# Where a two-layer hybrid kernel loads its modulation weights: token stores behind the first norm's weights, later modulation rows beside the second pair's features

## The chip, the cores and the metric

One Trainium2 chip, one core. The metric is the device time of one execution in microseconds, the median over several runs. Engine names are the profile's: PE is TensorE's matmul, PEld its weight load, DVE is VectorE, ACT ScalarE, POOL GpSimd, SP the engine whose queue issues every DMA of this kernel.

## What is computed

Two trunk layers work on 1024 latent and 256 context tokens of width 1024. In each layer a condition vector gives 3072 modulation numbers for the latent tokens and 3072 for the context (shift, scale, gate); the tokens are normalised and modulated, projected, mixed by a retention head group and an RWKV-7 head group, projected out, and added to the residual times the gate.

```python
def adaln(cond, w_mod, b_mod):
    m = jax.nn.silu(cond.astype(jnp.float32)) @ w_mod + b_mod
    return jnp.split(m, 3, axis=-1)
...
    for layer in range(DEPTH):
        sh_l, sc_l, g_l = adaln(c, w_mod[layer], b_mod[layer])
        sh_c, sc_c, g_c = adaln(c_ctx, w_mod[layer], b_mod[layer])
        hl = rms_norm(xl, norm_w[layer]) * (1.0 + sc_l[:, None]) + sh_l[:, None]
        hc = rms_norm(xc, norm_w[layer]) * (1.0 + sc_c) + sh_c
        pl = hl @ w_in[layer]
        pc = hc @ w_in[layer]
...
        xl = xl + g_l[:, None] * mix_l
```

`w_mod[layer]` is 1024 by 3072 float32, 12 MB; both layers' make 24 MB, in the kernel three blocks of 8 MB.

## The kernel before

Tokens lie as 10 tiles of 128 (tiles 0 and 1 are context). The kernel writes program order by hand, and a scheduler then moves instructions on each engine's queue: it starts what is ready in its own timeline and prefers what was written earlier, so an instruction may run well ahead of its place in the program. On the chip each engine works its queue in order.

**The modulation rows.** `adaln` (L270 to L295) multiplies the two condition vectors with one 8 MB block of `w_mod`. For each of 8 row blocks it loads a `wm` tile of 128x2048 (1 MB, L277) and makes four products of 2x512 into the bank `pmod` (L280); the profile shows each product as two passes. I call the four products of one `wm` tile a group. The four write different partitions of the bank and run side by side, so a group or half of one takes about the same time. Then `pmodT` (L289) turns the rows into columns. It is called three times: block one, shift and scale of layer 0, inside the first norm (L454); block two, the gates of both layers (L1145); block three, shift and scale of layer 1 (L1146). The `wm` tiles have three buffers (`WMB`).

**The start of layer 0.** Token tiles are loaded (`xt`, L167), transposed into `xs` (`pxt`, L451), and each of the three `xs` chunks is stored to DRAM once (`xd<-xs`, 1, 2 and 2 MB, L459), for the residual at the layer's end. `norm_chunk` (L341 to L365) writes the normalised tokens as two half-precision parts, `h_hi` and `h_lo`. Then `lora` (L682 to L691) projects 128 columns (`pproj`, L486 to L488: five pieces of 24 products), and `features(0)` (L734 to L784) projects the keys, receptances and values of the first head pair, with the `zstage` (`pz`, L696 to L724) merged into the receptances. Projection weights come through `w_block` (L322 to L334): a load `wraw`, two ACT passes and one POOL pass into `whi` and `wlo`, each with two buffers. Then the scan begins.

**The scan.** Four head pairs of ten steps make 40 steps a layer. `seq` (products `pseq`, L1044 and L1052) and the preparation `prep2` have high priority. Between the steps `deal` hands out other work from two streams: `stream` (features, gates and retention of the pairs, through `feats`) and `out_stream` (the output projection, `pout`). The pair `DENSE[l]` says how much work, in microseconds of PE, each stream holds; `deal` spreads it over the steps left.

Of the kernel before, what the change touches and what calls it, by code (L numbers as in the profile page):

```python
# [10 lines left out]
F32 = mybir.dt.float32  # L11
# [3 lines left out]
ALU = mybir.AluOpType  # L15
# [39 lines left out]
WMB = 3  # L55
# [1 line left out]
RETW = 32  # L57
NTM = (5, 7)
XB = 4
DENSE = ((447.0, 113.0), (403.0, 88.0))  # L60
DUE = (30, 37)


# [62 lines left out]
def hybrid_kernel(ctx: ExitStack, tc: tile.TileContext, a: dict, out: bass.AP, dbg: dict | None = None):  # L126
    nc = tc.nc
# [14 lines left out]
    def pj(name="pj"):  # L142
        return bank("pj", name)

    load = nc.sync.dma_start

    def behind(ins, first):
        tc.add_manual_dep(ins.ins, first.ins.name, mybir.DependencyInfo(mybir.DependencyClass.NoSync, mybir.DependencyReason.DATA),
                          reason="the first product of a bank clears its written bits")

    open_pools = {}

# [55 lines left out]
    at = {}  # L208
# [34 lines left out]
    x_v = x_d.rearrange("k p t -> p k t")  # L243
# [16 lines left out]
    silu = const.tile([128, 16], F32, name="silu")  # L260
# [6 lines left out]
        nc.vector.scalar_tensor_tensor(silu, th, 1.0, p[:, 0:16], ALU.add, ALU.mult)  # L267
        nc.vector.tensor_scalar(silu, silu, 0.5, None, ALU.mult)

    def adaln(pool, spans, tag):  # L270

        pt = bank(tag, "pmod")
        for k in range(8):
            wm = pool.tile([128, 2048], F32, tag="wm", name="wm", bufs=WMB)
            n = 0
            for l, b0, nb in spans:
                load(wm[:, 512 * n:512 * (n + nb)], a["w_mod"][l, 128 * k:128 * k + 128, 512 * b0:512 * (b0 + nb)])  # L277
                n += nb
            for n in range(4):
                nc.tensor.matmul(pt[32 * n:32 * n + 2, :], silu[:, k:16:8], wm[:, 512 * n:512 * n + 512],  # L280
                                 start=(k == 0), stop=(k == 7))
        ms = pool.tile([128, 512], F32, tag="ms", name="ms", bufs=2)
        nc.gpsimd.memset(ms, 0.0)
        for n in range(4):
            r = slice(32 * n, 32 * n + 2)
            (nc.scalar.copy if n % 2 else nc.vector.tensor_copy)(ms[r], pt[r])
        p2 = bank(tag, "pmodT")
        for j in range(4):
            nc.tensor.transpose(p2[:, 128 * j:128 * j + 128], ms[:, 128 * j:128 * j + 128], ident)  # L289
        n = 0  # L290
        for l, b0, nb in spans:
            v = p2.rearrange("p (j n c) -> p c n j", j=4, c=32)[:, 0:2, n:n + nb]
            n += nb
            for c in range(2):
                nc.vector.tensor_copy(modr[l][:, c, 4 * b0:4 * (b0 + nb)].rearrange("p (n j) -> p n j", j=4), v[:, c])  # L295

    def merge(x, nx, y, ny):

# [75 lines left out]
    for l in range(DEPTH):  # L374
# [55 lines left out]
        if l == 0:  # L430
            lp = ln_pool
            stage = [lp.tile([128, 8, 128 * len(tiles)], F32, name=f"xs{ci}") for ci, tiles in enumerate(LN_TILES)]
            for ci, tiles in enumerate(LN_TILES):
                nt = len(tiles)
                rs = lay.tile([128, 4], F32, tag=f"rs{ci}", name="rs")
                hs = lp.tile([128, 4, 2], F32, tag="hs", name="hs", bufs=2)
                rss[ci] = rs
                xt = []
                for i, tb in enumerate(tiles):
                    t = x_tiles[tb] if tb < XTB else x_tile(tb)  # L440
                    for q in range(2):
                        junk = lp.tile([128, 512], F32, tag="ntm", name="junk", bufs=NTM[0])
                        nc.scalar.activation(junk, t[:, 512 * q:512 * q + 512], AF.Square, accum_out=hs[:, i, q:q + 1])
                    xt.append(t)
                nc.vector.tensor_tensor(rs[:, 0:nt], hs[:, 0:nt, 0], hs[:, 0:nt, 1], ALU.add)
                nc.vector.tensor_scalar(rs[:, 0:nt], rs[:, 0:nt], 1.0 / D, EPS, ALU.mult, ALU.add)
                pow_mhalf(rs[:, 0:nt], rs[:, 0:nt])
                for k in range(8):
                    p = bank(("inv", "m")[k % 2], "pxt")
                    for i, t in enumerate(xt):  # L450
                        nc.tensor.transpose(p[:, 128 * i:128 * i + 128], t[:, 128 * k:128 * k + 128], ident)  # L451
                    (nc.scalar.copy if k % 2 else nc.vector.tensor_copy)(stage[ci][:, k, :], p[:, 0:128 * nt])
                if ci == 0:
                    adaln(lp, [(0, 0, 4)], "sq")  # L454
            mod = dict(A=modulation(8, 8, "A", True), B=modulation(0, 8, "B", False))
            for ci, tiles in enumerate(LN_TILES):
                norm_chunk(lp, l, h, mod, tiles, rss.pop(ci), lambda k: stage[ci][:, k, :])
            for tiles, x in zip(LN_TILES, stage):
                load(x_v[:, :, 128 * tiles[0]:128 * tiles[-1] + 128], x)  # L459
            lv32 = lp.tile([128, 768], F32, tag="xt", name="lv32", bufs=XTB)  # L460
            load(lv32, a["c_lv"])
            nc.vector.tensor_copy(lvm.rearrange("p d n t -> p (d n t)"), lv32)
        else:
            mod = dict(A=modulation(8, 8, "A", True), B=modulation(0, 8, "B", False))
            lp = open_pool("nm", side)
            for tiles in OUT_TILES:
                x = xres.pop(tiles[0])
                norm_chunk(lp, l, h, mod, tiles, rss.pop(tiles[0]), lambda k: x[:, k, :])
            close_pool("nm")
            close_pool("xl")  # L470
            close_pool("xa")
            close_pool("ow")
# [334 lines left out]
        def out_sum(x, tiles, k, parts):  # L807

            c = 1 if tiles[0] < 2 else 0
            p = pj("pout")[:, 0:128 * len(tiles)]  # L810
            for i, ((hi, lo), (mh, ml)) in enumerate(parts):
                nc.tensor.matmul(p, hi, mh, start=(i == 0), stop=False)  # L812
                nc.tensor.matmul(p, hi, ml, start=False, stop=False)  # L813
                nc.tensor.matmul(p, lo, mh, start=False, stop=(i == len(parts) - 1))  # L814
            nc.vector.scalar_tensor_tensor(x, p, gmod[:, c, k:k + 1], x, ALU.mult, ALU.add)

        def out_part(chunks, key, stay):

# [322 lines left out]

        for _ in lora():
            pass
        if l == 0:
            adaln(lp, [(0, 4, 2), (1, 4, 2)], "inv")  # L1145
            adaln(lp, [(1, 0, 4)], "sq")  # L1146
        for _ in features(0):
            pass
        if l == 0:
            close_pool("ln")  # L1150
        gmod = modulation(16, 8, "G", False)

        def feats(p):
            yield from gates(p)
            gated.add(p)
            if p + 1 < NP:
                yield from merge(zstage(p + 1), 4.3, features(p + 1), 44)
                ready.add(p + 1)
            else:
                yield from ret_keys(p, cs[p])  # L1160
# [38 lines left out]
        fills = [stream(), out_stream()]  # L1199
        left = list(DENSE[l])  # L1200

# [23 lines left out]
        sp = open_pool("scan", other)  # L1225
# [79 lines left out]
```

## Time and profile before

| | |
|---|---|
| median of 3 runs (lowest to highest) | 2474.76 us (2469.43 to 2476.56) |
| profiled execution, its own time | 2457.0 us |
| its span, first to last instruction | 2455.2 us |
| PE busy | 2291.1 us, 93% |
| VectorE busy | 1735.0 us, 71% |
| ScalarE busy | 1416.7 us, 58% |
| GpSimd busy | 1321.3 us, 54% |
| mean granted TensorE clock | 0.968 |
| HBM read, written | 212.21 MB, 85.98 MB |

Each row of a timeline has a start and a duration in microseconds, the engine, the line, what is written and read, the shape, and in brackets how long the engine had been idle before it and what ended that. A matmul's duration is its latency; matmuls overlap, so their rate is read from the distance of their starts. The granted clock is a share of full speed: 1.00 is 2.4 GHz, 0.50 is 1.2 GHz, and a mean between them is a mix of the two in time.

### The profile page before, as it was taken

What the parts mean: (1) busy time and instruction counts of PE and PEld (TensorE: products, weight loads), DVE (VectorE), ACT (ScalarE), POOL (GpSimd) and SP (SyncE); (2) the same over time, 40 slices, a digit from 0 to 9 for tenths busy, and PEclk for the clock granted to TensorE, in tenths of its full rate; (3) what the DMA queues carried; (4) which work ended last, traced back from release to release, by engine and by line L of the source; (5) the groups of instructions that cost most, each with busy time, mean ns of one, the idle gap of its engine ahead of it and who ended that gap; (6) DMA issues with size and microseconds to landing.
All of it is one profiled execution on the core that took longest, in us unless ns stands there. A gap on an engine that the chain in (4) does not pass through costs nothing.

```text
span 2455.2 us, 69588 instructions
## 1 busy us (share of the span) xinstructions
PE 2291.1 (93%) x25463; PEld 1730.3 (70%) x25463; DVE 1735.0 (71%) x4784; ACT 1416.7 (58%) x4261; POOL 1321.3 (54%) x2032
## 2 busy tenths in 40 slices
PE   5778999999999999999996899999999999998997
PEld 2357776877688777778655687678768867776855
DVE  2656676787678867787648678767867876768756
ACT  3455664565566655566546666646655665556663
POOL 1455564465546644556536566545654665456662
PEclk7889999999999999999998899999999999999999
DMA  8754343344334423346543544334433443234544
GB/s 309 270 191 116 112 119 85 110 111 127 79 87 133 134 68 94 76 110 163 160 123 108 155 126 115 105 94 119 126 87 102 124 115 85 75 96 120 143 131 129
DMA packets 539606, 302.77 MB, mean 123 GB/s; under 512 B 238995, under 2 KB 526465, under 8 KB 537217
## 3 DMA queue, kind: packets, MB, share of 16 engines
q1 hardware_dynamic: 539264, 298.33, 42.3%
q8 instruction: 201, 3.29, 0.6%
q14 instruction: 141, 1.15, 0.2%
HBM read 212.21 MB, written 85.98 MB: 121 GB/s over the span
## 4 chain that ended last, share of the span: by engine, by line
PE 63%; DVE 12%; DMA 5%; ACT 3%; issue 3%; POOL 2%; SPq 1%; DVEq 0%; POOLq 0%; ACTq 0%
PE pproj L486 9%; PE pproj L488 9%; PE pproj L487 8%; PE pseq L1052 8%; PE pm L953 5%; PE pinv L992 2%; PE pseq L1044 2%; PE pinv L1008 2%; PE pout L812 2%; PE pout L814 2%; PE pout L813 1%; PE pss L629 1%; PE pkt L588 1%; PE pss L639 1%; PE pbt L960 1%
## 5 line engine op out<-in xcount | busy, mean ns | idle before, releaser
L486 PE MATMUL pproj<-h_hi,whi 128*128 128x256 f16 (+2 forms) x2128 | 630.2, 298 | 14.0 <-ACT h_hi L364 8.5
L487 PE MATMUL pproj<-h_lo,whi 128*128 128x256 f16 (+2 forms) x2128 | 628.1, 297 | 6.1 <-DVE h_lo L365 5.6
L488 PE MATMUL pproj<-h_hi,wlo 128*128 128x256 f16 (+2 forms) x2128 | 626.9, 297 | 1.0 <-POOL wlo L320 1.0
L320 POOL TENSOR_TENSOR wlo<-wraw,whi 128x256 f16<-128x256 f32 x360 | 250.3, 707 | 210.2 <-ACT wraw L319 186.0
L486 PEld LDWEIGHTS <-whi 128*128 128x128 f16 x2128 | 212.5, 100 | 83.1 <-issue 18.8
L488 PEld LDWEIGHTS <-wlo 128*128 128x128 f16 x2128 | 213.2, 100 | 75.4 <-issue 10.9
L487 PEld LDWEIGHTS <-whi 128*128 128x128 f16 x2128 | 212.4, 100 | 74.7 <-issue 16.5
L977 POOL COPY ttb<-tt 64x256 f16<-64x256 f16 x320 | 139.0, 435 | 203.1 <-DVE tt L1012 155.7
L1006 DVE TENSOR_TENSOR xx<-pinv,lvm 128x256 f16<-128x256 f32 x400 | 163.8, 415 | 94.0 <-PE pinv L992 90.8
L318 ACT ACTIVATE whi<-wraw 128x256 f16<-128x256 f32 x360 | 138.8, 411 | 132.1 <-PE pproj L487 61.0
L1009 ACT CAST tz<-pinv 128x256 f16<-128x256 f32 x400 | 146.0, 371 | 117.2 <-PE pinv L1008 105.9
L953 PE MATMUL pm<-own,bk 64*128 64x128 f32 (+1 forms) x1280 | 198.9, 291 | 8.0 <-DVE bk L933 4.1
L1012 DVE STREAM_TRANSPOSE tt<-tz 128x256 f16<-128x256 f16 x320 | 139.3, 437 | 92.0 <-ACT tz L1009 87.3
L967 POOL TENSOR_TENSOR il<-gq,c_id 64x256 f32<-64x256 f32 x160 | 120.5, 753 | 133.3 <-DVE gq L956 114.7
L977 ACT COPY ttb<-tt 64x256 f16<-64x256 f16 x320 | 128.6, 402 | 101.3 <-DVE tt L1012 96.5
L953 PEld LDWEIGHTS pm<-own,bk 64*128 64x128 f32 x1280 | 160.8, 190 | 33.2 <-issue 9.5
L956 DVE TENSOR_TENSOR gq<-pm,c_m 128x256 f32<-128x256 f32 (+1 forms) x320 | 115.5, 401 | 47.7 <-PE pm L953 46.7
L1052 PE MATMUL pseq<-st,own 64*64 64x64 f32 x2432 | 148.9, 227 | 0.0
L319 ACT ACTIVATE wraw<-wraw 128x256 f32<-128x256 f32 x376 | 146.4, 410 | 3.9
L1003 POOL TENSOR_TENSOR lo<-il,hi 64x256 f16<-64x256 f32 x160 | 113.3, 708 | 35.9 <-ACT hi L968 24.8
L992 PEld LDWEIGHTS <-hi 128*128 128x128 f16 x1920 | 104.0, 99 | 39.6 <-issue 9.3
L1008 PE MATMUL pinv<-xx,ttb 128*128 128x64 f16 x1600 | 112.8, 194 | 11.7 <-DVE xx L1006 9.4
(255 smaller groups left out, 5897.9 us busy)
## 6 DMA issues: line engine op xcount, KB each, us to landing
ft<-feat SPq DMA_DIRECT2D x320, 160.0 KB
wraw<-in_w_in_dram SPq DMA_DIRECT2D x264, 128.0 KB
feat<-zth SPq DMA_DIRECT2D x80, 256.0 KB
wm<-in_w_mod_dram SPq DMA_DIRECT2D x16, 1024.0 KB
wraw<-in_w_out_dram SPq DMA_DIRECT2D x112, 128.0 KB
lap<-la SPq DMA_DIRECT2D x40, 256.0 KB
uv<-vt SPq DMA_DIRECT2D x320, 32.0 KB
wm<-in_w_mod_dram SPq DMA_DIRECT2D x16, 512.0 KB
```

The costliest lines, as they stand in the source:

```text
L319: nc.scalar.activation(raw, raw, AF.Copy, scale=WS)
L320: nc.gpsimd.tensor_tensor(lo, raw, hi, ALU.subtract)
L486: nc.tensor.matmul(p[:, 0:n], hi[:, k, :], h_hi[:, kk, m0:m1], start=first, stop=False)
L487: nc.tensor.matmul(p[:, 0:n], hi[:, k, :], h_lo[:, kk, m0:m1], start=False, stop=False)
L488: nc.tensor.matmul(p[:, 0:n], lo[:, k, :], h_hi[:, kk, m0:m1], start=False, stop=stop)
L953: nc.tensor.matmul(pm[h][:, i, d, 0:q1], bk[HR[h], i, d, :], own[HR[h], i, d, 0:q1], start=True, stop=True)
L977: eng(idr(dst[HR[h], :, :, 64 * h:64 * h + 64]), idr(src[HR[h]]))
L992: nc.tensor.matmul(q[:, i, d, :], hi[:, i, d, :], id16 if n == 0 else tz[:, i, d, :], start=True, stop=True)
L1006: nc.vector.tensor_tensor(xx, q, mk, ALU.mult)
L1008: nc.tensor.matmul(tp[:, i, d, :], ttb[:, i, d, :], xx[:, i, d, :], start=True, stop=True)
L1009: nc.scalar.copy(tzn, tp)
L1052: rm = nc.tensor.matmul(pq[HR[h], k, d, :], lhs, rhs, start=False, stop=stop, skip_group_check=True)
```

## The change

Two things move. The three stores of `xs` get an ordering to the last `pmod` product of block one, which concerns the order of the queue and adds no wait. Blocks two and three leave their place ahead of `features(0)` and become a generator, `gate_rows`, merged with the second pair's features; their `wm` tiles come from the scan's pool with two buffers instead of three, their bank is `rt` instead of `inv` and `sq`, and `modulation(16, ...)` (the gates) moves with them. `DENSE[0]` grows by the 9 units that the generator yields.

```diff
-DENSE = ((447.0, 113.0), (403.0, 88.0))
+DENSE = ((456.0, 113.0), (403.0, 88.0))
...
-    def adaln(pool, spans, tag):
+    def adaln(pool, spans, tag, bufs):
...
-            wm = pool.tile([128, 2048], F32, tag="wm", name="wm", bufs=WMB)
+            wm = pool.tile([128, 2048], F32, tag="wm", name="wm", bufs=bufs)
...
-                nc.tensor.matmul(pt[32 * n:32 * n + 2, :], silu[:, k:16:8], wm[:, 512 * n:512 * n + 512],
-                                 start=(k == 0), stop=(k == 7))
-        ms = pool.tile([128, 512], F32, tag="ms", name="ms", bufs=2)
+                at["pmod"] = nc.tensor.matmul(pt[32 * n:32 * n + 2, :], silu[:, k:16:8], wm[:, 512 * n:512 * n + 512],
+                                              start=(k == 0), stop=(k == 7))
+            yield 0.5
+        ms = pool.tile([128, 512], F32, tag="ms", name="ms", bufs=1)
...
             for tiles, x in zip(LN_TILES, stage):
-                load(x_v[:, :, 128 * tiles[0]:128 * tiles[-1] + 128], x)
+                behind(load(x_v[:, :, 128 * tiles[0]:128 * tiles[-1] + 128], x), at["pmod"],
+                       "the weights of the modulation go first")
...
-        if l == 0:
-            adaln(lp, [(0, 4, 2), (1, 4, 2)], "inv")
-            adaln(lp, [(1, 0, 4)], "sq")
         for _ in features(0):
             pass
         if l == 0:
             close_pool("ln")
-        gmod = modulation(16, 8, "G", False)
+        gmod = []
+
+        def gate_rows():
+
+            if l == 0:
+                yield from adaln(sp, [(0, 4, 2), (1, 4, 2)], "rt", 2)
+                yield from adaln(sp, [(1, 0, 4)], "rt", 2)
+            gmod.append(modulation(16, 8, "G", False))
...
-                yield from merge(zstage(p + 1), 4.3, features(p + 1), 44)
+                wide = merge(zstage(p + 1), 4.3, features(p + 1), 44)
+                yield from wide if p else merge(gate_rows(), 9 if l == 0 else 1, wide, 48)
```

The built order shows where the scheduler puts them. First, SP's queue in the first norm, before:

```order
L277 DMA wm<-in_w_mod_dram 128x2048
L167 DMA xt<-in_x_dram 128x1024 x2
L459 DMA xd<-xs_175 128x8x256
L277 DMA wm<-in_w_mod_dram 128x2048
```

and after the change, from the last four `wm` tiles of block one:

```order
L277 DMA wm<-in_w_mod_dram 128x2048 x2
L167 DMA xt<-in_x_dram 128x1024 x4
L334 DMA wraw<-in_w_in_dram 128x2x128
L462 DMA xd<-xs_175 128x8x256
L462 DMA xd<-xs_176 128x8x512
L465 DMA lv_565<-in_c_lv_dram 128x768
L462 DMA xd<-xs_177 128x8x512
L693 DMA la<-la 64x256 x4
L712 DMA lap<-la 128x2x256
L693 DMA la<-la 64x256 x4
L277 DMA wm<-in_w_mod_dram 128x1024 x4
```

The 1 MB store has gone from between the weights of block one to behind its last token tiles, and the first weights of block two stand behind the stores of `lora`'s first two pieces, where before six of its eight tiles stood ahead of them.

Second, PE's queue around block three. Before, its first groups follow block two in the middle of the key projection of `features(0)`:

```order
L280 MATMUL pmod<-wm,silu 2x512 x4
L289 MATMUL pmodT<-c_id,ms 128x128 x4
L280 MATMUL pmod<-wm,silu 2x512 x8
L486 LDWEIGHTS whi
L486 MATMUL pproj<-h_hi,whi 128x256
```

After, they stand in the receptance projection, among the `pks` products of the keys and the `pz` products:

```order
L290 MATMUL pmodT<-c_id,ms 128x128 x4
L756 MATMUL pks<-c_id,rn 64x128 x4
L280 MATMUL pmod<-wm,silu 2x512 x8
L749 MATMUL pks<-bones_111,psq 128x2 x2
L756 MATMUL pks<-c_id,rn 64x128 x4
L280 MATMUL pmod<-wm,silu 2x512 x4
L720 LDWEIGHTS wz
L720 MATMUL pz<-lh,wz 128x256
```

and the SP queue that feeds them is

```order
L277 DMA wm<-in_w_mod_dram 128x2048 x2
L712 DMA lap<-la 128x2x256
L760 DMA feat_115<-pkp 128x256
L727 DMA feat_115<-zth 128x2x256 x2
L760 DMA feat_115<-pkp 128x256
L277 DMA wm<-in_w_mod_dram 128x2048 x2
```

So block two now lies in the key projection and block three in the receptance projection of the first pair: later than before, yet still ahead of the first scan step but for one group, and not beside the second pair's features. Each `wm` load of block three stands behind stores of results that PE's own products make.

Third, PE's queue at the last `pseq` of layer 0. Before:

```order
L814 MATMUL pout<-mh,wll 128x512
L1052 MATMUL pseq<-uv,gq 64x64 x4
L881 MATMUL pxo<-c_id,x_18738 128x128
L812 LDWEIGHTS wlh
L812 MATMUL pout<-mh,wlh 128x512
```

After:

```order
L818 MATMUL pout<-mh,wll 128x512
L885 MATMUL pxo<-c_id,x_18738 128x128
L1056 MATMUL pseq<-uv,gq 64x64 x4
L885 MATMUL pxo<-c_id,x_18738 128x128
L816 LDWEIGHTS whi
L816 MATMUL pout<-mh,whi 128x256
```

Behind the last `pseq` and ahead of layer 1's first projection stood 120 `pout` products (96 of 128x256, 24 of 128x512); now 345 stand there (216 and 129), among them the main part of the output projection, which reads `whi`.

## Rows read from the trace of the kernel before

**Rows 1.** The page's parts 1 and 2: busy time, then slices of 61 us.

```profile
PE 2291.1 (93%) x25463; PEld 1730.3 (70%) x25463; DVE 1735.0 (71%) x4784; ACT 1416.7 (58%) x4261; POOL 1321.3 (54%) x2032
...
PE   5778999999999999999996899999999999998997
...
PEclk7889999999999999999998899999999999999999
```

**Rows 2.** Busy by stretch: PE, PEld, DVE, ACT, POOL; PEclk, DMA share, GB/s.

```profile
67.00:92.00 25.00, 18.31 (x88) 6.54 (x88) 24.84 (x29) 13.21 (x26) 20.52 (x15) 0.77 0.69 253
92.00:140.00 48.00, 43.44 (x318) 22.76 (x316) 17.32 (x37) 18.28 (x45) 7.95 (x11) 0.90 0.76 274
140.00:182.00 42.00, 29.77 (x214) 22.05 (x213) 23.88 (x53) 21.58 (x66) 25.55 (x45) 0.84 0.52 151
182.00:205.00 23.00, 18.73 (x161) 14.89 (x161) 17.66 (x35) 13.33 (x36) 15.46 (x22) 0.93 0.41 113
```

**Rows 3.** The same for tile pmod alone: PE, PEld, DVE, ACT; PEclk, DMA share, GB/s.

```profile
67.00:92.00 25.00, 9.73 (x28) 0.68 (x28) 0.00 (x0) 0.00 (x0) 0.77 0.69 253
92.00:140.00 48.00, 16.10 (x92) 1.55 (x92) 1.37 (x2) 1.16 (x2) 0.90 0.76 274
140.00:182.00 42.00, 1.04 (x8) 0.11 (x8) 1.37 (x2) 1.16 (x2) 0.84 0.52 151
```

**Rows 4.** PE's waits from 20 to 60 us: total, times, longest.

```profile
PE pmod L280 <- DMA wm<-in_w_mod_dram: 12.2, 4, 5.3
```

**Rows 5.** Busy by stretch, all engines, a slice of the first norm.

```profile
20.00:40.00 20.00, 12.67 (x62) 5.01 (x61) 4.41 (x9) 7.26 (x19) 2.94 (x4) 0.74 0.95 323
```

**Rows 6.** Timeline of the SP queue: the first store, two late weight loads.

```profile
25.53 0.65 SPq L459 DMA_DIRECT2D xd<-xs  x1
...
111.34 1.02 SPq L277 DMA_DIRECT2D wm<-in_w_mod_dram  x2
```

**Rows 7.** Timeline of PE: projection products at two rates, and pmod groups.

```profile
93.08 0.42 PE L487 MATMUL pproj<-h_lo,whi 128*128 128x258 f16 x1
93.29 0.42 PE L488 MATMUL pproj<-h_hi,wlo 128*128 128x258 f16 x1
...
105.62 0.27 PE L487 MATMUL pproj<-h_lo,whi 128*128 128x258 f16 x1
105.73 0.27 PE L488 MATMUL pproj<-h_hi,wlo 128*128 128x258 f16 x1
...
107.56 1.03 PE L280 MATMUL pmod<-wm,silu 128*2 128x512 f32 x4
...
112.35 1.04 PE L280 MATMUL pmod<-wm,silu 128*2 128x512 f32 x8
...
116.67 1.04 PE L280 MATMUL pmod<-wm,silu 128*2 128x512 f32 x8 [2.69 <-DMA wm<-in_w_mod_dram]
119.58 1.89 PE L280 MATMUL pmod<-wm,silu 128*2 128x512 f32 x8 [1.87 <-DMA wm<-in_w_mod_dram]
```

**Rows 8.** Timeline of VectorE: the end of the first norm.

```profile
97.72 1.40 DVE L365 SCALAR_TENSOR_TENSOR h_lo<-ntm,modB,h_hi 128x512 f16<-128x512 f32 x2
```

**Rows 9.** Timeline of ACT: the key projection's second half of weights.

```profile
119.89 0.42 ACT L318 ACTIVATE whi<-wraw 128x256 f16<-128x256 f32 x1 [7.79 <-DMA wraw<-in_w_in_dram]
```

**Rows 10.** PE's waits from 140 to 180 us: total, times, longest.

```profile
PE pks L752 <- POOL rn L250: 2.5, 2, 1.4
PE pz L716 <- ACT lh L711: 2.3, 1, 2.3
```

**Rows 11.** Busy by stretch, all engines: the scan, and the layer boundary.

```profile
700.00:800.00 100.00, 100.00 (x1221) 83.00 (x1220) 83.21 (x237) 61.37 (x177) 59.76 (x83) 1.00 0.43 121
...
1290.00:1340.00 50.00, 30.30 (x246) 25.68 (x245) 45.35 (x103) 33.68 (x105) 32.59 (x52) 0.83 0.33 106
```

**Rows 12.** Timeline of PE: the last two half steps of layer 1's scan.

```profile
2411.82 0.45 PE L1044 MATMUL pseq<-uv,gq 128*64 128x64 f32 x8
...
2417.58 0.45 PE L1044 MATMUL pseq<-uv,gq 128*64 128x64 f32 x8
```

More of the change, by code (lines that the diff above doesn't have):

```diff
@@ L145, in hybrid_kernel, with behind @@
     load = nc.sync.dma_start
-    def behind(ins, first):
+    def behind(ins, first, why="the first product of a bank clears its written bits"):
         tc.add_manual_dep(ins.ins, first.ins.name, mybir.DependencyInfo(mybir.DependencyClass.NoSync, mybir.DependencyReason.DATA),
-                          reason="the first product of a bank clears its written bits")
+                          reason=why)
     open_pools = {}
@@ L295, in adaln @@
                 nc.vector.tensor_copy(modr[l][:, c, 4 * b0:4 * (b0 + nb)].rearrange("p (n j) -> p n j", j=4), v[:, c])
+        yield 0.5
     def merge(x, nx, y, ny):
@@ L453, in hybrid_kernel @@
                 if ci == 0:
-                    adaln(lp, [(0, 0, 4)], "sq")
+                    for _ in adaln(lp, [(0, 0, 4)], "sq", WMB):
+                        pass
             mod = dict(A=modulation(8, 8, "A", True), B=modulation(0, 8, "B", False))
@@ L814, in out_sum @@
                 nc.tensor.matmul(p, lo, mh, start=False, stop=(i == len(parts) - 1))
-            nc.vector.scalar_tensor_tensor(x, p, gmod[:, c, k:k + 1], x, ALU.mult, ALU.add)
+            nc.vector.scalar_tensor_tensor(x, p, gmod[0][:, c, k:k + 1], x, ALU.mult, ALU.add)
         def out_part(chunks, key, stay):
```

## The prediction

> **What bounds the kernel now.** I read the page first, then the busy times by stretch, the waits, and the timelines of the start. The page shows a kernel that PE bounds: 93% busy, nine tenths or more in nearly every slice from the fifth on, and full clock there [rows 1]. Inside the scan PE is busy 100 of 100 us [rows 11]. Work that is only shifted there costs what it gives. Three places are not full: the first three slices, the layer boundary and the end. This change works in the first.
>
> The start has three stretches. Up to 67 us the chip waits for bytes: from 20 to 40 us the DMA engines are 95% busy at 323 GB/s [rows 5], and PE waits 12.2 us for `wm` between 20 and 60 us [rows 4]. From 67 to 92 us VectorE is the bound, 24.84 of 25 us, in the norm [rows 2]; its last pieces end at 99 us [rows 8]. From 92 us PE works through `lora` and the features of pair 0 until the first scan step at 205 us, with 4.6 us idle to 140, 12.2 us to 182 and 4.3 us to 205 (stretch less busy time) [rows 2].
>
> The products of blocks two and three lie in these stretches: 9.73 us before 92, 16.10 us from 92 to 140, 1.04 us after [rows 3]. The first part is free today, since it runs beside VectorE's norm; the second stands in PE's way.
>
> **The change part by part.** I sum the shift of the first scan step, minus being earlier.
>
> (a) *The store behind the weights.* The 1 MB store is issued at 25.53 us [rows 6], ahead of four of block one's weight tiles. At 323 GB/s [rows 5] its 1.05 MB take 3.2 us, and the norm waits for those weights. Gain 3.2 us, or none if the token tiles, which also come later, hold the norm. The queue was full, so I take **-3.2**. The stores end long before anything reads them, at the layer's end; `lora`'s stores behind them are ready only near 90 us.
>
> (b) *The moved products lose their free place.* After 92 us stand 17.1 us of them now (16.10 + 1.04) [rows 3]. After the change all stand there. A group takes 1.04 us at full clock, a half 1.03 [rows 7]. In the built order the sixteen groups, split ones included, form 19 separate runs, so 19 x 1.04 = 19.8 us; at the mixed clock of today all together took 26.9 us. So +2.7 to +9.7; I take **+6**, the middle, because the granted clock from 92 to 182 us lies between the levels (0.90, 0.84) [rows 2].
>
> (c) *Waits for weights that go.* In the key projection PE waited 2.69 and 1.87 us for `wm` of block three [rows 7], and ACT 7.79 us for the key weights that were queued behind those megabytes [rows 9]; in the built order these key weights come first. Gain 4.6 us at least as PE shows it, 7.8 at most. I take **-4.6**, since ACT's wait ran beside PE's groups.
>
> (d) *Block three falls into idle time.* Its eight runs, 8.3 us, now stand in and behind the receptance projection, where PE is idle 16.5 us (12.2 + 4.3) [rows 2] in waits of 1 to 2.3 us for POOL and ACT [rows 10]. PE's queue is in order, so a group fills a wait if its weights are there and it stands just ahead of the waiting product. Between 0 and 8.3 us are absorbed; about half of the runs stand beside `pks` and `pz` products, the ones that wait, so I take **-5**.
>
> (e) *New waits with two buffers.* A load issued at 111.34 us reached its product at 116.67, 5.3 us later, and the second at 119.58, 8.2 us later [rows 6, 7]. With two buffers the load of group n+2 is issued after the product of group n, and SP works in order, so it also waits for the stores ahead of it. Where 24 projection products lie between (24 x 0.11 = 2.6 us at the starts of 105.62 and 105.73 [rows 7]) most of it is covered; between the second and third groups of block three lie six short products only. Bounds: 0, and four pairs of groups that each expose 5.3 less about 1.5 us of work, 15 us. I take **+3**: one exposed load in full, less its share of waits that PE has there anyway.
>
> The sum is -3.2 + 6 - 4.6 - 5 + 3 = -3.8 us, say **-4 us** at the first scan step. One group and its transposes stand behind that step, counted among the 19 runs.
>
> *The scan.* PE is full there [rows 11], so the shift is carried to the end. The fill is handed out differently: at the end of layer 0 the built order leaves 120 products of 128x256 and 105 of 128x512 more behind the last step, 120 x 0.11 + 105 x 0.22 = 36 us of PE work (the larger at twice the smaller's cost). It is the same work, later; it costs only if steps run dry. A half step with little beside it takes 5.8 us [rows 12], a step 11.5. By my count the last three steps keep some 31 us of fill and about 11 us of `pseq`, above 34.6 us together, but one has only 9 us, hence 2.5 us idle at most. At the boundary PE is idle 19.7 of 50 us [rows 11], on VectorE's norm, untouched. I take 0, with 5 us either way. The single `ms` buffer, the gate rows' later addition and `DENSE` are covered by PE's fill; their worth is in these bounds.
>
> The profiled execution took 2457.0 us, so 2453 on its scale. The median of the runs shown is 2474.76, 17.8 us above it; the difference applies there: 2474.8 - 4 = **2471 us**. A measurement of this kernel can tell about 0.3%, 7.4 us, from no change.
>
> **The rivals.**
>
> *The start is latency, and the groups vanish in it.* For it: from 140 to 205 us PE is idle 16.5 of 65 us in short waits [rows 2, 10], and ACT had 7.8 us of waiting for key weights [rows 9]. Then (b) is +2.7, (c) -7.8, (d) -8.3, (e) up to 5: with (a) -3.2 between -12 and -17 us, likeliest **2462 us**. Against it: the groups need their own loads in time.
>
> *The two buffers starve PE in the receptance projection (slower).* Place: the SP queue, where block three's loads stand behind stores of `pkp`, `zth` and `prc`, results of PE's own last products, while PE's next group stands ahead of the `pz` products and the first `pm` of the scan's preparation. Price: (e) at 15 instead of 3 and (d) at -2: -3.2 + 6 - 4.6 - 2 + 15 = +11, **2486 us**. It decides from the point where PE's waits for `wm` after 100 us exceed about 7 us. Against it: 24 products lie between half of the groups. The Trainium skill, "DMA: Bandwidth & Descriptors", in its section on the anatomy of one DMA, says that a DMA engine doesn't wait on semaphores, the issuing sequencer does, before dispatch; by that every late store would hold the loads behind it, which is this case.
>
> *The clock.* Without the early groups PE has 8.6 us of other work from 67 to 92 us (18.31 - 9.73) [rows 2, 3]. Today the granted clock there is 0.77, and at 93 us products start 0.21 us apart, at 105 us 0.11 [rows 7]. If `lora`'s 70 products after 92 us all run at the slow rate instead of a fifth of them, that costs 56 x 0.10 = 6 us: **2477 us**. The Trainium skill, "TensorE: Matmul & The Clock Gate", Part 1, states that the throttled state is the default and activity releases it; that rule speaks against taking products out of a half-empty stretch, and the 0.77 agrees with it.
>
> *The change does not do what it says.* The built order keeps all but one group ahead of the scan. Truly beside the second pair they would cost 19.8 us of a full PE and free 17.1 + 4.6 + 3.2 = 24.9: -5 us, the same number. So it has no chance of its own.
>
> **How the numbers follow.** Forecast 0.44, vanishing groups 0.28, starved buffers 0.18, clock 0.10. The likeliest time is 2471; the forecast's own range is 2464 to 2478. The vanishing case and the scan's 5 us give the low end, 2457, the starved case at +11 the high end, 2486. Faster by over 0.3% (below 2467): most of the 0.28 and a fifth of the forecast, 0.36. Slower by over 0.3% (above 2482): three quarters of the starved case and a little of the clock's and the forecast's, 0.17. Within: 0.47.
>
> **What would show it.** The norm's first VectorE row 3 us earlier shows (a); no `pmod` row between 60 and 92 us and `lora` done 5 to 9 us sooner shows (b) and (c); PE's wait list from 100 to 200 us shows (e), a few microseconds of `wm` in the forecast and over 7 in the slower rival; the first `pseq` near 201 us shows the sum, near 191 the faster rival. The granted clock from 67 to 110 us tests the clock. I am wrong about the scan if its length from first to last `pseq` differs by more than 5 us.

## The result, and the profile after

The changed kernel is slower: 2490.11 us median of 18 runs (2477.32 to 2499.89) against 2468.07 us of 18 runs of the kernel before (2451.87 to 2477.36). The ratio is 1.0104, 95% interval 1.0087 to 1.0120, so 22 us more where 4 less were predicted.

| profiled execution | before | after |
|---|---|---|
| its time, us | 2457.0 | 2481.4 |
| span, us | 2455.2 | 2479.2 |
| mean granted TensorE clock | 0.968 | 0.957 |
| first `pseq` product | 205.45 | 200.25 |
| first `pseq` of layer 1 | 1418.91 | 1440.16 |
| last `pseq` | 2421.11 | 2441.87 |

The last three rows part the 24.0 us of the two spans: the start gives 5.2 us, layer 0 from its first scan product to layer 1's first takes 26.5 us more (1239.9 against 1213.5), layer 1's scan takes the same (1001.7 and 1002.2), and the end behind it 3.2 us more (37.3 and 34.1).

The first scan product came 5.2 us earlier, where 4 were forecast. Busy by stretch after, the first three of the stretches of [rows 2], with their columns:

```profile
67.00:92.00 25.00, 14.01 (x69) 8.59 (x67) 25.00 (x28) 12.99 (x24) 18.72 (x14) 0.64 0.12 35
92.00:140.00 48.00, 40.06 (x302) 24.22 (x301) 15.25 (x32) 20.62 (x62) 17.89 (x37) 0.96 0.70 231
140.00:182.00 42.00, 31.14 (x229) 16.22 (x228) 20.06 (x47) 17.72 (x48) 15.92 (x18) 0.88 0.98 323
```

The same for tile `pmod` alone, as in [rows 3]:

```profile
67.00:92.00 25.00, 0.00 (x0) 0.00 (x0) 0.00 (x0) 0.00 (x0) 0.64 0.12 35
92.00:140.00 48.00, 10.79 (x52) 1.08 (x52) 0.00 (x0) 0.00 (x0) 0.96 0.70 231
140.00:182.00 42.00, 11.51 (x68) 1.08 (x68) 1.37 (x2) 1.15 (x2) 0.88 0.98 323
```

No `pmod` product is left between 67 and 92 us, and the clock there is 0.64 instead of 0.77; behind 92 us stand 23.3 us of them (10.79 + 11.51, and 1.04 from 182 to 205 us), where 17.1 stood.

The loss is in the second half of layer 0. Two stretches of PE, before and then after (columns: stretch, its length, PE busy with its matmuls, granted clock, DMA share, GB/s):

```profile
1000.00:1250.00 250.00, 240.20 (x2895) 0.99 0.45 126
1250.00:1450.00 200.00, 166.09 (x1468) 0.91 0.46 133
```

```profile
1000.00:1250.00 250.00, 235.22 (x2762) 0.90 0.43 120
1250.00:1450.00 200.00, 170.02 (x1348) 0.89 0.44 127
```

Idle time hardly differs: 9.8 + 33.9 us before, 14.8 + 30.0 after, 1.1 us more. But time spent working at a low clock is lost too: busy time times (1 - clock), an estimate of it, is 2.4 + 14.9 us before and 23.5 + 18.7 after, 24.9 us more. The two make 26 us, the whole loss between these two profiles. In steps of 10 us, after:

```profile
1030.00:1040.00 10.00, 8.03 (x97) 0.72 0.37 85
1040.00:1050.00 10.00, 10.00 (x90) 0.50 0.24 67
1050.00:1060.00 10.00, 10.00 (x63) 0.76 0.11 31
1060.00:1070.00 10.00, 10.00 (x128) 1.00 0.77 197
1070.00:1080.00 10.00, 7.95 (x102) 0.94 0.25 75
1080.00:1090.00 10.00, 10.00 (x93) 0.55 0.39 93
1210.00:1220.00 10.00, 7.28 (x116) 0.93 0.93 322
1220.00:1230.00 10.00, 7.03 (x67) 0.50 0.66 210
1230.00:1240.00 10.00, 9.18 (x60) 0.54 0.40 113
```

Three times the clock falls to its lower level of 1.2 GHz, and after the first two falls it stays there while PE is busy 10 of 10 us. Before, the same stretches stand at 0.95 or more; three of them:

```profile
1040.00:1050.00 10.00, 9.98 (x126) 1.00 0.31 87
1080.00:1090.00 10.00, 10.00 (x154) 1.00 0.31 85
1220.00:1230.00 10.00, 10.00 (x97) 1.00 0.19 55
```

What PE did ahead of the first fall and around the second, from the timeline of after (the bracket is the idle time before the product, and who ended it), then the first fall by the microsecond:

```profile
1030.27 0.66 PE L643 MATMUL pss<-vtk,smk 128*128 128x64 f32 x4 [0.37 <-DVE ob L640]
1031.53 0.45 PE L1056 MATMUL pseq<-uv,bt 128*64 128x64 f32 x8 [0.37 <-DVE uv L1076]
1034.07 0.42 PE L659 MATMUL pot<-c_id,ob 128*128 128x128 f32 x2 [1.29 <-DVE ob L656]
...
1079.17 0.37 PE L996 MATMUL pinv<-tz,hi 128*128 128x64 f16 x4 [1.99 <-DVE tz L999]
```

```profile
1032.00:1033.00 1.00, 0.78 (x21) 1.00 1.16 259
1033.00:1034.00 1.00, 0.00 (x0) 1.00 0.89 169
1034.00:1035.00 1.00, 0.89 (x9) 0.66 0.08 17
1035.00:1036.00 1.00, 1.00 (x14) 0.50 0.01 3
...
1054.00:1055.00 1.00, 1.00 (x4) 0.60 0.00 0
1055.00:1056.00 1.00, 1.00 (x6) 1.00 0.00 0
```

PE waits 0.37, 0.37 and 1.29 us, and then works 20 us at 0.50. The fall at 1078.7 us comes within a single wait of 1.99 us, for a VectorE result, and lasts 10 us. While PE waits there, VectorE works through operations of the retention fill (`lgc`, `qt`) and of the preparation of a later step (`bk`) that stand ahead of the scan's `tz` in its queue:

```profile
1076.51 0.87 DVE L514 COPY lgc<-lgb 64x8 f32<-64x8 f32 x2
1077.41 0.51 DVE L528 TENSOR_TENSOR qt<-qt,ropec 128x256 f32<-128x256 f32 x1
1077.84 0.41 DVE L1010 TENSOR_TENSOR xx<-pinv,lvm 128x256 f16<-128x256 f32 x1
1078.18 0.60 DVE L937 TENSOR_TENSOR bk<-ft,bk 128x256 f32<-128x256 f32 x1
1078.71 0.41 DVE L999 TENSOR_TENSOR tz<-pinv,lvm 128x256 f16<-128x256 f32 x1
```

The third fall, at 1218.6 us, looks different: PE is busy 7.28 of 10 us there, with several waits for ScalarE and VectorE, none over 0.9 us, and 7.03 and 9.18 of 10 us behind it.

### The profile page after: what moved, and what is told of

Read it like the earlier page. It is cut to its first block, busy times and chain, and to the rows that moved or that the text cites. A ratio compares the mean times of both kernels' runs of the same rounds, so it can differ in the third digit from the quotient of the medians.

```text
span 2479.2 us, 69534 instructions
## 1 busy us (share of the span) xinstructions
PE 2306.2 (93%) x25463; PEld 1750.5 (71%) x25463; DVE 1707.6 (69%) x4784; ACT 1412.5 (57%) x4261; POOL 1326.6 (54%) x2032
## 5 line engine op out<-in xcount | busy, mean ns | idle before, releaser
L490 PE MATMUL pproj<-h_hi,whi 128*128 128x256 f16 (+2 forms) x2128 | 630.1, 298 | 14.8 <-ACT whi L320 4.0
L1003 POOL TENSOR_TENSOR ttb<-hi,lvm 128x256 f16<-128x256 f16 x160 | 114.2, 733 | 12.1 <-ACT hi L972 11.1
```

The source lines that it names most:

```text
L490: nc.tensor.matmul(p[:, 0:n], hi[:, k, :], h_hi[:, kk, m0:m1], start=first, stop=False)
```

## The experiments

The first theory (A): the loss is the clock, which falls where a new order of the fill lays short waits together. Its rivals: (B) the out projection's products, which now stand behind layer 0's last scan step, leave its last steps too thin; (C) the moved rows or the held stores themselves cost. Times are medians in us, and each ratio is to the runs of the kernel before on the same chip, with its 95% interval.

**One part at a time.** Four kernels: the kernel before with the stores held and nothing else; before with the other table and nothing else; the change without its table; the change without the hold.

```diff
 hold_only: before, and
-                load(x_v[...], x)
+                behind(load(x_v[...], x), at["pmod"])
 dense_456_only: before, and
-DENSE = ((447.0, 113.0), ...
+DENSE = ((456.0, 113.0), ...
 after_447: after, and the same line the other way
 after_no_hold: after, and
-                behind(load(x_v[...], x), at["pmod"], ...)
+                load(x_v[...], x)
```

> The kernel before, with only the three token stores held behind the products of the first modulation block; blocks two and three stay where they were, and the table of densities is the old one. Theory A (the loss is TensorE time at the half clock in layer 0's scan, after short waits that the new order of the fill lays close together): the first scan step comes 3 us earlier than before's 205.45 (about 202), the fill and its order in layer 0 are almost those of before, the granted clock between 1000 and 1240 stays at 1.00 as before, and the time is 2465 (before less 3), mean granted clock 0.966 to 0.970. Theory B (the loss is output work left behind layer 0's last scan step): the out projection's products behind that step are those of before (36,864 columns, 15.7 us of work), so 2465 too. Theory C (the held stores themselves cost, because the gathers of the tokens come later): 2480 or more, first layer-0 scan step earlier but waits for token tiles later.

> The kernel before with nothing but the density 447 changed to 456: no store held, no block moved, only the handing out of the fill in layer 0 differs. Theory A: the first scan step stays at 205.5; the order of the fill is another, so the granted clock falls at other places; the time differs from before's by the work lost at the half clock alone, anywhere from -5 to +30 us, and the mean granted clock tells how much (0.01 of it is about 12 us). Theory B: 61,440 columns of the out projection stand behind layer 0's last scan step instead of 36,864, which is 10 us more work there; the time rises by 0 to 10 us with the granted clock as before. Theory C: no change, 2468.

> The changed kernel with the density put back from 456 to 447. Theory A: another order of the fill, so other falls of the clock; the first scan step stays at 200.2; the time is that of after less or plus the difference of half-clock work, 2460 to 2500, and goes with the mean granted clock (0.968 would give about 2463). Theory B: 165,376 columns of the out projection stand behind layer 0's last scan step (70 us of work, where after has 121,344, 52 us), so it is slower than after by 10 to 18 us: 2500 to 2508. Theory C: as after, 2490.

> The changed kernel without the hold on the token stores; the rows of gates and of the next layer stay beside the second pair's features, the density stays 456. Theory A: the first scan step comes about 3 us later than after's 200.2; the order of the fill moves a little, the falls of the clock move with it, 2465 to 2500, and the time goes with the mean granted clock. Theory B: the work behind layer 0's last scan step is that of after (122,880 columns), so 2493. Theory C: the stores alone are the cost, so the time falls to before's 2468.

| | median (runs) | ratio | clock 1000 to 1250 us |
|---|---|---|---|
| hold_only | 2460.52 (12) | 0.9973 (0.9953 to 0.9993) | 0.96 |
| dense_456_only | 2488.59 (6) | 1.0085 (1.0056 to 1.0114) | 0.92 |
| after_447 | 2487.14 (8) | 1.0074 (1.0048 to 1.0101) | 0.92 |
| after_no_hold | 2480.68 (12) | 1.0070 (1.0047 to 1.0094) | 0.95 |

The hold alone is a gain of some 5 us (its clock from 1000 to 1250 us was 0.96, where theory A expected 1.00). The table alone, with no row moved and no store held, costs as much as the whole change, though TensorE's list in the profile is that of before up to 1065 us, its first 10,822 of 25,463 products. So C isn't needed for a loss of this size. It isn't refuted either: after_447 differs from hold_only by the moved rows alone (and the lists that come with them), and it is 27 us slower. Putting the table back in the changed kernel doesn't help, and after_447, with the most work behind the last step, isn't slower than after: that speaks against B. Within a kernel the time goes with the mean granted clock: over the runs of all kernels of this study, 0.01 of clock is 19 us (the expectation's 12 was too low). Between kernels the clock isn't all: brought to a clock of 0.96 at that price, the mean of before's runs is 2470 us, of after's 2475, but of after_early's 2485, after_mid's 2491 and full_c's (below) 2484.

**More or less work behind the last step.** Other tables for the changed kernel, and one that spoils the hold kernel.

```diff
 after_early:  after,     DENSE[0] = (475.0, 125.0), DUE = (29, 35)
 after_mid:    after,     DENSE[0] = (475.0, 113.0), DUE = (29, 35)
 after_due36:  after,     DENSE[0] = (456.0, 113.0), DUE = (30, 36)
 hold_late:    hold_only, DENSE[0] = (430.0, 113.0), DUE = (30, 38)
```

> The changed kernel with another table: densities 475 and 125 for 456 and 113, due at steps 29 and 35 for 30 and 37, so that the out projection's products go in beside the last scan steps of layer 0. Behind its last step stand 30,720 columns of them (13 us of work; after 121,344, 52 us; before 36,864, 16 us); the first scan step is that of after. Theory B (steps with too little fill run at the scan's own latency, so work moved behind the last step is paid twice): time 2460 to 2466, the stretch from the last step of layer 0 to the first of layer 1 about 168 us (before 170, after 203), median clock 0.961 or more. Theory A (any other order of the fill has its own falls of the clock, without regard to how much stands behind): 2465 to 2500 with a clock of 0.950 to 0.960. Theory C (the moved rows cost): 2490.

> The changed kernel with densities 475 and 113 and due at steps 29 and 35: 70,656 columns of the out projection behind the last step of layer 0 (30 us). Theory B: between the two, 2470 to 2478, last step of layer 0 to first of layer 1 about 182 us. Theory A: 2465 to 2500, without regard to the order of the amounts. Theory C: 2490.

> The changed kernel with the second due step 36 for 37 alone; the fill is the same up to step 33, and 87,552 columns of the out projection stand behind the last step of layer 0 (37 us). Theory B: 2475 to 2483 (15 us less work behind the last step than after), last step of layer 0 to first of layer 1 about 188 us. Theory A: 2465 to 2500. Theory C: 2490.

> The kernel before with the stores held (2460.5 in its run), with the density 447 lowered to 430 and the second due step put to 38, so that 165,888 columns of the out projection (70 us of work) stand behind the last step of layer 0 in place of 36,864; no row of gates is moved. Theory B: slower by 20 to 30 us, 2480 to 2490, last step of layer 0 to first of layer 1 about 222 us, clock 0.95. Theory A: 2450 to 2490, no relation to the amount behind. Theory C: 2460, nothing of the modulation is moved.

| | columns behind | median (runs) | ratio | clock 1000 to 1250 us |
|---|---|---|---|---|
| after_early | 30,720 | 2495.40 (4) | 1.0125 (1.0088 to 1.0163) | 0.92 |
| after_mid | 70,656 | 2493.16 (4) | 1.0124 (1.0087 to 1.0162) | 0.94 |
| after_due36 | 87,552 | 2491.17 (4) | 1.0110 (1.0076 to 1.0143) | 0.91 |
| hold_late | 165,888 | 2486.11 (9) | 1.0082 (1.0054 to 1.0110) | 0.94 |

Taken alone, hold_late came out in B's range (and far from C's 2460). But B falls on the other three: the least work behind gives the slowest kernel of the four. The profiles show why. From the last `pseq` of layer 0 to the first of layer 1 after takes 181.1 us, after_due36 162.6, after_mid 157.8 and after_early 136.4, so this stretch shrinks, as B said, by 18, 23 and 45 us. But the scan ahead of it, from first to last `pseq` of layer 0, grows by 14, 30 and 52 us (from 1058.8 to 1072.6, 1088.4 and 1110.8). Work behind the step is moved, not paid twice, as the prediction said.

**Thin steps, or a picked table.** Two new theories: T, the last six steps need enough fill; S, the table 447 was picked, and any other is worse. Four other tables on the hold kernel.

```diff
 full_a:   hold_only, DENSE[0] = (453.0, 120.0), DUE = (30, 36)
 full_b:   hold_only, DENSE[0] = (447.0, 113.0), DUE = (29, 36)
 full_c:   hold_only, DENSE[0] = (465.0, 125.0), DUE = (30, 36)
 hold_450: hold_only, DENSE[0] = (450.0, 113.0), DUE = (30, 37)
```

> The kernel before with the stores held (2460.5 in its run) and another table: densities 453 and 120, due at 30 and 36, for 447 and 113, 30 and 37. TensorE's order is that of the hold kernel up to product row 12,076 of its list (about 1060 us); behind it the last six steps of layer 0 hold 96 us of fill, as there. Theory T (what costs is too little fill beside those six steps: TensorE then waits for the scan's own chain, and the clock falls): 2455 to 2466, clock 0.962 or more. Theory S (the table 447, 113 was picked among many for its order, and any other order has more falls, whatever it holds): 2475 to 2490, clock 0.950 to 0.956.

> The kernel before with the stores held, densities as before, due at 29 and 36 for 30 and 37: the order is another from row 11,073 (about 960 us) on, the last six steps of layer 0 hold 111 us of fill, and 23,040 columns of the out projection stand behind them (10 us). Theory T: 2450 to 2462, clock 0.962 or more. Theory S: 2475 to 2490, clock 0.950 to 0.956.

> The kernel before with the stores held, densities 465 and 125, due at 30 and 36: the order is another from row 6,356 (about 530 us) on, the last six steps of layer 0 hold 90 us of fill. Theory T: 2458 to 2468, clock 0.960 or more. Theory S: 2475 to 2490, clock 0.950 to 0.956.

> The kernel before with the stores held and the density 447 put to 450 alone: TensorE's order is that of the hold kernel up to row 12,076, like that of the first kernel of this batch, but the last six steps of layer 0 hold 85 us of fill (96 there), and 61,440 columns of the out projection stand behind them (26 us of work). Theory T: 2475 to 2485. Theory S: 2475 to 2490 too; so it tells the two apart only beside the first kernel of this batch. That neither holds, and the first change of the table's run was chance: 2460.

full_a 2473.10 (12 runs, ratio 1.0039, 1.0020 to 1.0058), full_b 2479.06 (8, 1.0062, 1.0038 to 1.0085), full_c 2476.53 (12, 1.0053, 1.0028 to 1.0078), and hold_450 2449.34 (12, 0.9948, 0.9924 to 0.9972). T misses all four. S meets two medians (full_b and full_c, at a higher clock than it said, 0.962 and 0.964), and both theories fall on the last: the kernel with the thinner steps, and with another table, is the fastest of all, 15 us under before. From 314 to 1387 us of its profile, all of layer 0 but the first 115 us of its scan, TensorE's list in it is, product by product, that of dense_456_only, which took 39 us more (in the profiles 32, of which layer 0 takes 30). So neither the amount of fill nor its order on TensorE in layer 0's scan settles the time.

**The same lists.** What can differ is when the waits fall. Three kernels have dense_456_only's list on TensorE in both layers, or differ from it only ahead of the scan; a fourth has that of after_no_hold, but for some products ahead of 40 us.

```diff
 same_list_hold2: before, DENSE[0][0] = 450.0, stores behind the 2nd group of block one
 same_list_hold6: before, DENSE[0][0] = 450.0, stores behind the 6th group
 before_450:      before, DENSE[0][0] = 450.0
 after_hold4:     after,  stores behind the 4th group of block one
```

> The kernel before with density 450, and the token stores held behind the second of the eight product groups of the first modulation block (not the last). TensorE's list is that of the kernel with density 456 alone (2488.6 us, clock 0.952) in all of the program, and the first scan step starts within some 3 us of its. Theory L (the lists decide): 2482 to 2495, clock 0.950 to 0.956. Theory M (the moments at which the short waits fall decide, which any shift before moves): anywhere between 2448 and 2492, with the clock (0.01 of it about 18 us).

> The same with the stores held behind the sixth group. TensorE's list differs from that of the density-456 kernel before the scan only (59 of the first 1,500 products stand elsewhere); the first scan step starts some 3 us earlier. Theory L: 2479 to 2492, clock 0.950 to 0.956. Theory M: anywhere between 2448 and 2492, not at the time of the run before but by chance.

> The kernel before with density 450 and no hold: the lists of TensorE, VectorE, ScalarE and GpSimd are instruction for instruction those of the density-456 kernel; only SyncE's transfers stand in another order from the 593rd of 1,347 on. Theory L: 2488 within 4, clock 0.952. Theory M: as that kernel or not, 2448 to 2492.

> The changed kernel with the stores held behind the fourth group of the first block instead of the last. TensorE's list is that of the changed kernel without the hold (2480.7, clock 0.9565). Theory L: 2478 to 2484. Theory M: 2455 to 2500.

Medians: same_list_hold2 2473.87 (6 runs, ratio 1.0052, 1.0032 to 1.0072), same_list_hold6 2485.70 (5, 1.0086, 1.0054 to 1.0117), before_450 2485.89 (6, 1.0078, 1.0037 to 1.0118), after_hold4 2476.10 (6, 1.0062, 1.0036 to 1.0089). Two lie inside the range of theory L, two under it, by 8 and 2 us; all four lie in the wide ranges of theory M. With so few runs each (2465 to 2496 in before_450 alone) the medians decide neither way. The profiles say more. The same three waits at the same place of the list, from the timeline of dense_456_only, with a `pseq` product ahead of them and the same one two half steps on, and the clock behind them:

```profile
1028.66 0.45 PE L1052 MATMUL pseq<-w,z 64*64 64x64 f32 x8
...
1030.28 0.28 PE L992 MATMUL pinv<-tz,hi 128*128 128x64 f16 x4 [0.59 <-ACT tz L1009]
1033.01 0.28 PE L981 MATMUL pinv<-tt,one 128*128 128x256 f16 x1 [0.76 <-DVE tt L1019]
1034.09 0.27 PE L981 MATMUL pinv<-tt,one 128*128 128x256 f16 x1 [0.56 <-ACT z L1028]
...
1054.81 0.32 PE L1052 MATMUL pseq<-w,z 64*64 64x64 f32 x2
```

```profile
1040.00:1050.00 10.00, 10.00 (x78) 0.50 0.28 80
```

The timeline of same_list_hold2, and its clock:

```profile
1036.40 0.45 PE L1054 MATMUL pseq<-w,z 64*64 64x64 f32 x8
...
1038.02 0.28 PE L994 MATMUL pinv<-tz,hi 128*128 128x64 f16 x4 [0.60 <-ACT tz L1011]
1040.75 0.28 PE L983 MATMUL pinv<-tt,one 128*128 128x256 f16 x1 [0.76 <-DVE tt L1021]
1041.83 0.27 PE L983 MATMUL pinv<-tt,one 128*128 128x256 f16 x1 [0.56 <-ACT z L1030]
...
1055.14 0.32 PE L1054 MATMUL pseq<-w,z 64*64 64x64 f32 x2
```

```profile
1040.00:1050.00 10.00, 8.66 (x141) 1.00 0.19 52
```

The waits are equal to 0.01 us, and in one execution the clock falls, in the other not; the kernel before has these waits too, at 1034.65, 1037.37 and 1038.45 us, and no fall behind them in its profile. This also prices a fall. From the `pseq<-w,z` products ahead of the waits to those two half steps on dense_456_only takes 26.1 us (1028.66 to 1054.81), same_list_hold2 18.7 us (1036.40 to 1055.14), and before 18.7 us as well (1033.03 to 1051.76). The clock stood at 0.50 for some 17 us of the 26.1. So 17 us at the half clock cost 7.4 us of time, with the same products and the same waits on PE. Over all of layer 0, first `pseq` to layer 1's first, the two profiles of this list with a clock of 0.92 and 0.91 from 1000 to 1250 us took 1233 and 1239 us, the two with 1.00 and 0.99 took 1221 and 1224.

**The two ends once more.**

> The hold kernel with density 450 once more, unchanged. If its lists are what makes it fast: 2445 to 2454, clock 0.968 or more, no half clock between 1000 and 1250 again. If it was the best of many by chance: 2455 to 2470, with one or more falls there.

> The changed kernel once more, unchanged. If its lists lay the waits together: 2486 to 2494, clock 0.950 to 0.956, and falls at about 1034, 1078 and 1218 us again, 40 to 50 us of half clock between 1000 and 1250. If the falls are thrown anew in every run: the same median, but other places and 0 to 50 us of half clock there.

hold_450_again took 2455.83 (10 runs), ratio 0.9943 (0.9919 to 0.9967); its clock from 1000 to 1250 us was 0.95 this time, with a fall behind those same three waits. By its own expectation that is the case of chance, by 1 us in the time and also by the clock (median 0.965) and the falls: part of the 15 us was luck, 12 us under before remain. after_again took 2485.88 (12 runs), ratio 1.0065 (1.0042 to 1.0089), and its first two falls came at the same waits again; its timeline, and its clock behind the first:

```profile
1038.29 0.41 PE L659 MATMUL pot<-c_id,ob 128*128 128x128 f32 x2 [1.28 <-DVE ob L656]
...
1083.49 0.37 PE L996 MATMUL pinv<-tz,hi 128*128 128x64 f16 x4 [1.98 <-DVE tz L999]
```

```profile
1040.00:1050.00 10.00, 10.00 (x97) 0.50 0.11 32
```

It had two falls more, at 1120 and 1158 us, which the first profile didn't have, and one at 1233 where that had 1218; 68 us of half clock in all from 1000 to 1250, where the first had 51. So neither of its expectations holds as a whole: two places came back, the third and the amount did not. after_due36, whose list is that of after up to 1072 us and which has both waits too (1.29 and 2.08 us), fell at both. So at these two waits the clock fell in three profiles of three, and behind the three waits of before's list in five of nine: hold_only, dense_456_only, before_450, full_a and hold_450_again, but not before, hold_450, same_list_hold2 and same_list_hold6.

## Why the prediction was wrong

It said 2471 us, 2457 to 2486; the time was 2490, on the side that it gave 0.17. Its base was high besides: the median of 18 runs of before is 2468.1, not the 2474.8 of three, so on that scale its forecast is 2464 and the miss 26 us.

- **The start was right in its sum.** The first `pseq` of this profile stands 5.2 us earlier, for the forecast of 4. (a) Block one's copies of its results begin at 48.48 us where they began at 51.78, 3.3 us earlier for the 3.2 forecast, and the norm's last piece ends 2.1 us earlier (97.06 against 99.12). (b) The products behind 92 us grew by 6.2 us (23.3 less 17.1) for the 6 taken. (d) PE's idle time from 140 us to the first `pseq` fell from 16.5 to 11.6 us, for the 5 taken. (c) did not come: ScalarE waits for the key weights as long as before, 7.78 us for 7.79, and PE 3.3 us behind it. With the stores held alone (hold_only) such waits do shrink, to 1.60 us on ScalarE and 0.8 us for `wm`. (e) PE's waits for `wm` from 100 to 200 us are 5.2 us in four, where they were 4.6 in two, so the starved-buffer rival, which needed 7, did not come. ScalarE's wait:

```profile
114.56 0.42 ACT L320 ACTIVATE whi<-wraw 128x256 f16<-128x256 f32 x1 [7.78 <-DMA wraw<-in_w_in_dram]
```

- **That sum was in part luck.** What made up for (c) is a term that the sum lacks, the clock: from 140 us to the first `pseq` it was 0.92, for 0.87 before; from 92 us on that is worth some 6 us by the estimate above. In the five other profiles of changed kernels with the same TensorE list up to there it was 0.84 to 0.86, and the first `pseq` stands at 201.6 to 205.1. The mean of the six is 202.7 us. The three with before's early list and no store held stand at 202.4 to 205.5, mean 204.3, and the seven with the stores held behind the whole block and no row moved at 196.9 to 202.8, mean 199.8. So by the means the hold gave some 4.4 us at the first step, and the moved rows took some 3 of them back.

- **The clock rival named the right resource in the wrong place.** The clock from 67 to 92 us did fall, from 0.77 to 0.64, but no slower start followed: `lora`'s stretch from 92 to 140 us had a clock of 0.96, for 0.90 before.
- **The step that failed** is *the scan*: "PE is full there, so the shift is carried to the end", with 0 for the fill that is handed out differently, 5 us either way, "hence 2.5 us idle at most". From first to last `pseq` the changed kernel takes 2241.6 us, before 2215.7, 26 us more. As idle time the guess was fair: 5.0 us more from 1000 to 1250 us, 3.9 less to 1450. As work it is the same: among the changed kernels those with more of it behind the last step were not the slower ones. What it left out, by taking a full PE for a PE at full clock, is that a wait's price isn't its length: ahead of each of the first two falls stood waits of 2.0 us in all, and the clock stayed down for 20 and 10 us in a stretch that PE fills. Those two, the third fall and a little more at the boundary make the 25 us. Why the clock falls at one such wait and not at another stays open.
- **The other omission:** the change rewrites the lists of both layers. The end behind the last `pseq` is 34.1 us in before and 34.1 and 34.0 in the two profiles of hold_450, and 37 to 43 in every other profile of this study, the changed kernel's 37.3 among them; in layer 1 the change itself moves nothing but the reading of the gates, and dense_456_only, which moves nothing there, has 39.0 us. That is 3 of the 24 us.

What is shown: where the time of the two profiles went (the clock from 1000 to 1250 us), which waits stand at the first two falls, what one fall costs, and that the hold gains with the old table and with 450 (in the changed kernel it doesn't: 1.0070 without it, 1.0104 and 1.0065 with it). What is only argued: that the gap of the medians, 22 us, is made by falls as the profiles' 24 us is; the clock of the runs supports it (median 0.952 in after, 0.963 in the later runs of before, at 19 us per 0.01 21 us; the 5 us that stay between 2475 and 2470 at an equal clock it does not explain). Open: the eight kernels with the rows moved, the repeat among them, all lie above before, 2476 to 2495, while the hold and table variants without them go from 2449 to 2489. Their profiles also have more idle time on PE from 1000 to 1250 us, 14.8 to 22.1 us against 9.6 to 17.2 in the twelve others. No run tells whether moving the rows brings this or only the lists it happened to get.

A kernel that beats both came out of it: the stores held, the rows left where they were, and 450 for 447, with 0.9948 and 0.9943 of before's time in two series.

## What to carry to other kernels

Where an engine's own queue fills a stretch, work and idle time alone don't price a change of the order: read the granted clock by 10 us over the whole span, for a few short waits can cost four times their length (1.9 us of them 7.4 us here). When an edit moves instructions in lists that a scheduler writes, count on a spread of over 1% from the lists and their moments (0.9943 to 1.0086 of before's time for a density of 447, 450 or 456, with and without the held stores), and price it by trying such neutral edits before crediting or blaming the edit itself. A part that gains alone (the held stores) should be timed alone before it is shipped with one that doesn't.

## What was not expected of the hardware

- The clock fell at waits of 1.3 us (with two of 0.37 us ahead of it) and 2.0 us in a stretch where PE was otherwise busy, and then stayed at the lower level for 20 and 10 us although PE was busy 10 of 10 us. The Trainium skill's page "TensorE: Matmul & The Clock Gate", under "A second HAM failure mode: psum-queue depth-cycling", describes frequent micro-idles of PE between groups that make the clock swing. The trace agrees with it in that short waits of PE went with falls (1.3 and 2.0 us), here waits for VectorE's results; it differs in that the second fall came at a single wait, without frequent ones.
- The same three waits, equal to 0.01 us, took the clock down in one profile and left it in another. So the fall isn't settled by PE's list and its waits as the profile shows them; what else settles it the runs don't show.
